# Weight halves at one fixed offset for each kind of stage, in place of offsets that cycle through eight

## The chip, the cores and the metric

The kernel runs on one core of a Trainium2 chip. What counts is the device time of one execution in microseconds (us), taken as the median of several runs. A separate execution is recorded by the hardware profiler; all rows come from that one.

## The reference

One encoder block over 272 token rows (16 learned ones ahead of 256 real ones) of width 2048, in float32:

```python
u = rmsnorm(h, ffn1_pre_g); h = h + 0.5 * rmsnorm(swiglu(u, w_gate, w_up, w_down), ffn1_post_g)
u = rmsnorm(h, mix_pre_g)
z = u @ w_in + b_in                       # 2048 x 9224: both mixers' inputs and two gates
br_m = (sigmoid(mo) * head_rmsnorm(mlstm(q, k, v, i, f))) @ m_w_branch
br_a = head_rmsnorm(diff_attention(aq, ak, av)) @ a_w_branch
h = h + rmsnorm((sigmoid(gm) * br_m + sigmoid(ga) * br_a) @ w_out, mix_post_g)
u = rmsnorm(h, ffn2_pre_g); h = h + 0.5 * rmsnorm(swiglu(u, ...), ffn2_post_g)
return h[:, 16:]
```

The feed-forward width is 5632. Nearly all the work is matrix products of the token rows with weights that are each used once.

## The kernel before

**Float32 products in three passes.** Every weight and every activation is split into a high half H (a copy that TensorE can multiply exactly) and a low half L = value - H. A product is H x XH + H x XL + L x XH. `product` (L202) issues it in one of two forms. Where the rows are 272 wide, three matmuls: L210 (H, XH), L211 (H, XL), L212 (L, XH). Where they are 256 wide and XH and XL lie side by side, two: one 512 wide with H (L215, L217) and one 256 wide with L (L214, L218). The 128 x 128 weight block is loaded anew for each matmul (the PEld rows).

**Units.** The weights come as 377 units of 128 x 2048 values (1 MB), in the order of their use. `load_unit` (L146) fetches the next one by DMA into one of three W tiles (L155), copies its two halves of 1024 columns with ScalarE into H tiles (L166) and lets VectorE subtract for the L tiles (L167). H and L have four tiles each, two of them per unit, so the next unit is split while TensorE works on the present one. A unit holds 16 products: 48 matmuls in the first form, 32 in the second. TensorE takes units strictly in order, so unit n begins with the first matmul of lines L210 to L218 after those of the units before it, and its stretch is read from there to the first matmul of the next.

**Where the halves lie.** An H or L tile is 1088 float32 values a partition (4352 bytes, 17 x 256), of which a unit uses 1024. Where in the tile they start is set by `phase(u)` (L80): for unit u the high half starts at 32 x (u mod 8) bytes and the low one at 32 x ((u + 2 x (u div 8)) mod 8) bytes. A pair of starts comes back every 32 units. The weight blocks within a unit are 512 bytes apart. The rows they meet have pitches that are whole multiples of 256 bytes: 576 values in U (L108), 320 or 256 values in the cells of the feed-forward's middle (L371) and 256 in the mixers' outputs HM and HA (L476, L800). So within one unit the distance from weights to rows is constant, counted modulo 256 bytes. Three small unused tiles (GAPS, L77, L103) set where the pools begin.

**Stages in order.** First feed-forward, 272 rows: 4 units that accumulate four blocks at once (`group`, L237), 44 single blocks (`block`, L267), 24 units of the down projection, 40 blocks, 20 units down. Mixer: 4 units, 5 + 24 blocks on 272 rows and 16 on 256, 8 units of the first branch (`branch`, L733), 32 gate blocks, 8 units of the second branch, 16 for the output projection. Second feed-forward, 256 rows: 4, 44, 24, 40 and 20 units. In the mixer the small matmuls of the attention and the matrix memory are put between units (`advance`).

Of the kernel before, what the change touches and what calls it, by code (L numbers as in the profile page):

```python
# [29 lines left out]
D, SEQ, META, DFF = 2048, 256, 16, 5632  # L30
T = META + SEQ
KT = D // 128
# [44 lines left out]
GAPS = (32, 40, 8)  # L77


def phase(u):  # L80
    h, l = u % 8, (u + 2 * (u // 8)) % 8
    return 8 * h, 8 * l

# [2 lines left out]
def block_kernel(ctx: ExitStack, tc: tile.TileContext, ht_d, w_d, vec_d, con_d, gc_d, out_d):  # L88
# [10 lines left out]
    def f(ap):  # L99
        return ap.bitcast(F32)  # L100
# [40 lines left out]
    def behind(ins, prev):  # L141
        tc.add_manual_dep(ins.ins, prev.ins.name,
                          mybir.DependencyInfo(mybir.DependencyClass.NoSync,
                                               mybir.DependencyReason.DATA), reason="issue order")

    def load_unit(parts=1, hold=None, dma=None):  # L146
        pieces = max(parts, st["pieces"])
        u = unit_no[0]
        unit_no[0] += 1
        W = sp.tile([128, 2048], F32, name="W", bufs=3)  # L150
        hp, lp = phase(u)
        n = 2048 // parts
        for i in range(parts):
            s = slice(i * n, (i + 1) * n)
            st["dma"] = nc.sync.dma_start(W[:, s], w_d[u, :, s])  # L155
            if dma:
                dma(i)
        HL = []
        for i in range(2):
            H = sp.tile([128, 1088], F32R, name="H", bufs=4)[:, hp:hp + 1024]  # L160
            L = sp.tile([128, 1088], F32R, name="L", bufs=4)[:, lp:lp + 1024]
            n = 2048 // pieces
            for o in range(0, 1024, n):
                s = slice(o, o + n)
                w = W[:, 1024 * i + o:1024 * i + o + n]
                a = nc.scalar.activation(H[:, s], w, AF.Copy)  # L166
                b = nc.vector.tensor_sub(L[:, s], w, f(H[:, s]))  # L167
                q = (1024 * i + o) // n
                if hold and hold[q % len(hold)]:
                    for x, y in zip((a, b), hold[q % len(hold)]):  # L170
                        behind(x, y)
            HL.append((H, L))
        return HL

# [7 lines left out]
    def bank(tag):  # L182
        return pp.tile([128, 512], F32, tag=tag, name=tag, bufs=BANKS[tag])

    def mm(cycle=1):
        tag = CYCLE[psn[0] % cycle]
        psn[0] += 1
        return bank(tag)
# [12 lines left out]

    def product(ps, HL, o, X, first, last):  # L202
        turn[0] = False if first else not turn[0]
        H, L = HL[o // 1024]
        o %= 1024
        H, L = H[:, o:o + 128], L[:, o:o + 128]
        XH, XL, both = X
        n = XH.shape[-1]
        if both is None:
            nc.tensor.matmul(ps[:, :n], H, XH, start=first, stop=False)  # L210
            nc.tensor.matmul(ps[:, :n], H, XL, start=False, stop=False)  # L211
            st["mm"] = nc.tensor.matmul(ps[:, :n], L, XH, start=False, stop=last)  # L212
        elif last or turn[0]:
            nc.tensor.matmul(ps[:, :n], L, XH, start=False, stop=False)  # L214
            st["mm"] = nc.tensor.matmul(ps[:, :2 * n], H, both, start=False, stop=last)  # L215
        else:
            nc.tensor.matmul(ps[:, :2 * n], H, both, start=first, stop=False)  # L217
            st["mm"] = nc.tensor.matmul(ps[:, :n], L, XH, start=False, stop=False)  # L218

    def halves(ps, X):  # L220
        n = X[0][0].shape[-1]
        return [ps[:, :n]] if X[0][2] is None else [ps[:, :n], ps[:, n:2 * n]]

    def plain(X):
        return [(h, l, None) for h, l, _ in X]
# [10 lines left out]

    def group(X, nk, n, tail=False, cycle=8, after=None, feed=None):  # L237
        pss = [mm(cycle) for _ in range(4)]
        Xb = [plain(X) if feed else X] * 4
        if tail:  # L240
            Xb[3] = plain(X)
        nu = nk // 4
        splits = []
        st["splits"] = splits
        for u in range(nu):
            if feed:
                hold = None
                if u == 1 and not feed.dma:
                    hold = [(st["square"],)] * 2 + [splits[2]] * 2
                elif u:  # L250
                    hold = [splits[4 * u - 2]]
                HL = load_unit(4 if u < 2 or feed.dma else 1, hold,
                               feed.dma(u) if feed.dma else None)
                splits += [feed(k) for k in range(4 * u, 4 * u + 4)]
            else:
                HL = load_unit()
            order = [(k, b) for k in range(4) for b in range(4)]
            if tail and u == nu - 1:
                order = [(k, b) for b in range(4) for k in range(4)]
            for k, b in order:  # L260
                kk = u * 4 + k
                product(pss[b], HL, k * 512 + b * 128, Xb[b][kk], kk == 0, kk == nk - 1)
                if tail and u == nu - 1 and k == 3 and after:
                    after(b, halves(pss[b], Xb[b]))
        return [halves(p, x) for p, x in zip(pss, Xb)]

    def block(X, cycle=1):  # L267
        ps = mm(cycle)
        HL = load_unit()
        for k in range(KT):  # L270
            product(ps, HL, k * 128, X[k], k == 0, k == KT - 1)
        return halves(ps, X)
# [56 lines left out]
    def residual(yg, r, cols, n, g):  # L329
        def feed(k):  # L330
            if k == 6:
                st["late"]()
            t = tmp()
            a = nc.vector.tensor_mul(t[:, :n], yg[:, k], r[:, :n])
            b = nc.vector.tensor_add(hT[:, k, cols], hT[:, k, cols], t[:, :n])
            if k == 0:
                st["first"] = b
            elif k == 1:
                behind(a, st["first"])
            return prenorm_operand(k, g, cols)  # L340
        feed.dma = None
        return feed
# [21 lines left out]
    def ffn(cols, n, post, feed):  # L364
# [28 lines left out]
        def pair(j):  # L393
            sg = gate(block(X, 8))
            up(j, sg, block(X, 8))

        def down(chunk, nk):
            for g in range(4):
                last = chunk == 1

                def finish(b, ps):
                    k = 4 * g + b
                    for p in ps:
                        nc.vector.tensor_add(Y[:, k], p, Y[:, k])
                    add_square(state["acc"], Y[:, k], n, k)
                    post_scale(Y, k, post)

                pss = group(F, nk, n, tail=last, after=finish if last else None)
                if not last:
                    for b in range(4):  # L410
                        total(Y[:, 4 * g + b], pss[b])

        psn[0] = 0
        pss = group(X, KT, n, feed=feed)
        pss += [block(X, 8) for _ in range(2)]
        state["r"] = rstd_of(prenorm_sum(cols, n), n, "rpre")
        pss.append(block(X, 8))
# [25 lines left out]
    def feed(k):  # L443
        return prenorm_operand(k, "f1pre", ALL)
# [13 lines left out]
    feed = residual(Y, r, ALL, T, "mpre")  # L458
# [274 lines left out]
    def branch(X, finish):  # L733
        for b2 in range(8):
            advance()
            HL = load_unit()
            pss = [mm(4), mm(4)]
            for k in range(8):
                for b in range(2):
                    product(pss[b], HL, k * 256 + b * 128, (X[:, k, 0], X[:, k, 1], X[:, k]),  # L740
                            k == 0, k == 7)
            for b in range(2):
                finish(2 * b2 + b, [pss[b][:, :SEQ], pss[b][:, SEQ:]])

    wide = {"mq", "mk", "mv", "ak", "av"}
# [12 lines left out]
    def advance():  # L758
        with tc.issue_after(st["mm"].ins):
            for g in list(waiting):  # L760
                if next(g, "end") == "end":
                    waiting.remove(g)
            if units:
                begin(units.pop(0))
# [5 lines left out]

    psn[0] = 0
    pss = group(XA, KT, T, feed=feed)
    pss += [start_block(i, 8) for i in (4, 5)]
    st["r"] = rstd_of(prenorm_sum(ALL, T), T, "rpre")
# [13 lines left out]
    def keep(j, ps):  # L788
        total(tm[:, j], ps)

    branch(HM, keep)
    gz = view(slot("G0", SLOTS["G0"], F32), 0, KT, SEQ)
    run(base["gm"], base["ga"])
# [35 lines left out]
    feed = residual(Y2, r, REAL, SEQ, "f2pre")  # L829
# [8 lines left out]
    for k in (2, 0, 6, 4, 10, 8, 12, 14):  # L838
        y, h = Y[:, k:k + 2], hT[:, k:k + 2, REAL]
# [163 lines left out]
```

## Time and profile before

| | us |
|---|---|
| median of 3 runs | 2299.19 (2296.04 to 2299.42) |
| profiled execution | 2298.4 |
| its span, first to last instruction | 2296.5 |
| TensorE matmuls busy | 2279.1 (99%) |
| TensorE weight loads busy | 2101.2 (91%) |
| VectorE busy | 1420.2 (62%) |
| ScalarE busy | 1160.5 (51%) |

Some 1.9 us lie around the span. The mean granted TensorE clock is 0.996 of full speed. A matmul's row shows from its start to its modelled end, and successive ones overlap: a 272-wide one is shown as 289 ns long while the next starts some 125 ns later. What a unit costs is therefore read from starts, not from busy time.

### The profile page before, as it was taken

What the parts mean: (1) busy time and instruction counts of PE and PEld (TensorE: products, weight loads), DVE (VectorE), ACT (ScalarE), POOL (GpSimd) and SP (SyncE); (2) the same over time, 40 slices, a digit from 0 to 9 for tenths busy, and PEclk for the clock granted to TensorE, in tenths of its full rate; (3) what the DMA queues carried; (4) which work ended last, traced back from release to release, by engine and by line L of the source; (5) the groups of instructions that cost most, each with busy time, mean ns of one, the idle gap of its engine ahead of it and who ended that gap; (6) DMA issues with size and microseconds to landing.
All of it is one profiled execution on the core that took longest, in us unless ns stands there. A gap on an engine that the chain in (4) does not pass through costs nothing.

```text
span 2296.5 us, 37068 instructions
## 1 busy us (share of the span) xinstructions
PE 2279.1 (99%) x15325; PEld 2101.2 (91%) x15325; DVE 1420.2 (62%) x2470; ACT 1160.5 (51%) x1869; POOL 0.8 (0%) x5
## 2 busy tenths in 40 slices
PE   9999999999999999999999999999999999999998
PEld 9999999999999998988987888888888888888897
DVE  7555544455555496488588757668666544666655
ACT  6444433444444465555569655556454444454444
POOL 0000000000000000000000000000000000000000
PEclk9999999999999999999999999999999999999999
DMA  7544444544454544434443455545555555555553
GB/s 255 176 179 177 173 181 169 182 168 183 167 183 165 195 178 147 172 123 166 165 147 129 183 184 184 191 157 186 193 189 184 189 193 186 184 186 192 191 184 110
DMA packets 61529, 404.56 MB, mean 176 GB/s; under 512 B 6704, under 2 KB 8880, under 8 KB 14000
## 3 DMA queue, kind: packets, MB, share of 16 engines
q1 hardware_dynamic: 61216, 400.33, 48.7%
q8 instruction: 120, 1.97, 0.3%
q0 software_dynamic: 144, 1.87, 0.2%
q14 instruction: 49, 0.40, 0.0%
HBM read 400.07 MB, written 2.10 MB: 175 GB/s over the span
## 4 chain that ended last, share of the span: by engine, by line
PE 98%; DVE 1%; DMA 0%; ACT 0%; issue 0%; SPq 0%; DVEq 0%
PE mm L215 10%; PE mm L217 10%; PE mm L210 7%; PE mm L212 7%; PE mm L211 7%; PE aux L210 6%; PE aux L212 6%; PE aux L211 6%; PE aux L215 5%; PE aux L217 5%; PE mm L214 5%; PE mm L218 5%; PE aux L214 3%; PE aux L218 3%; PE vt L212 2%; PE vt L211 2%
## 5 line engine op out<-in xcount | busy, mean ns | idle before, releaser
L167 DVE TENSOR_TENSOR L<-W,H 128x1024 fp32r<-128x1024 f32 (+1 forms) x866 | 935.1, 1085 | 610.2 <-ACT H L166 599.3
L166 ACT ACTIVATE H<-W 128x1024 fp32r<-128x1024 f32 (+1 forms) x866 | 812.1, 946 | 768.7 <-PE aux L211 214.6
L210 PE MATMUL mm<-U,H 128*128 128x272 f32 (+1 forms) x1056 | 306.2, 291 | 8.3 <-ACT U L321 7.9
L212 PE MATMUL mm<-U,L 128*128 128x272 f32 (+1 forms) x1056 | 304.4, 289 | 0.4 <-DVE L L167 0.4
L211 PE MATMUL mm<-U,H 128*128 128x272 f32 (+1 forms) x1056 | 304.6, 289 | 0.0
L217 PE MATMUL mm<-U,H 128*128 128x512 f32 x728 | 289.3, 398 | 0.0
L215 PE MATMUL mm<-U,H 128*128 128x512 f32 x728 | 288.2, 396 | 0.0
L210 PE MATMUL aux<-U,H 128*128 128x272 f32 x752 | 217.1, 289 | 0.0
L211 PE MATMUL aux<-U,H 128*128 128x272 f32 x752 | 216.3, 288 | 0.0
L212 PE MATMUL aux<-U,L 128*128 128x272 f32 x752 | 216.2, 288 | 0.0
L210 PEld LDWEIGHTS mm<-U,H 128*128 128x128 f32 x1056 | 199.1, 189 | 10.2 <-ACT U L321 9.2
L214 PE MATMUL mm<-U,L 128*128 128x256 f32 x728 | 205.4, 282 | 0.0
L218 PE MATMUL mm<-U,L 128*128 128x256 f32 x728 | 205.0, 282 | 0.0
L211 PEld LDWEIGHTS mm<-U,H 128*128 128x128 f32 x1056 | 200.0, 189 | 0.8 <-DVE U L322 0.2
L212 PEld LDWEIGHTS mm<-U,L 128*128 128x128 f32 x1056 | 199.7, 189 | 0.9 <-DVE L L167 0.9
L214 PEld LDWEIGHTS mm<-U,L 128*128 128x128 f32 x728 | 137.2, 188 | 32.8 <-issue 0.4
L218 PEld LDWEIGHTS mm<-U,L 128*128 128x128 f32 x728 | 137.3, 189 | 32.0 <-issue 0.7
L217 PE MATMUL aux<-U,H 128*128 128x512 f32 x367 | 145.1, 395 | 0.0
L212 PEld LDWEIGHTS aux<-U,L 128*128 128x128 f32 x752 | 141.7, 188 | 0.0
L211 PEld LDWEIGHTS aux<-U,H 128*128 128x128 f32 x752 | 141.6, 188 | 0.1
L210 PEld LDWEIGHTS aux<-U,H 128*128 128x128 f32 x752 | 141.3, 188 | 0.1
L215 PE MATMUL aux<-U,H 128*128 128x512 f32 x353 | 139.2, 394 | 0.0
(272 smaller groups left out, 4420.3 us busy)
## 6 DMA issues: line engine op xcount, KB each, us to landing
W<-in_w_dram SPq DMA_DIRECT2D x369, 1024.0 KB, 4.8
W<-in_w_dram SPq DMA_DIRECT2D x32, 256.0 KB, 5.3
out_dram<-hT SPq DMA_DIRECT2D x8, 256.0 KB, 2.4
G<-in_gc_dram POOLq DMA_DIRECT2D x1, 1824.0 KB, 8.0
hT<-in_h_dram SPq DMA_DIRECT2D x6, 272.0 KB, 5.4
hT<-in_h_dram SPq DMA_DIRECT2D x1, 544.0 KB, 6.6
con<-in_con_dram SPq DMA_DIRECT2D x1, 528.0 KB, 5.8
vec<-in_vec_dram SPq DMA_DIRECT2D x1, 118.5 KB, 2.0
```

What stands on the lines that cost most here:

```text
L166: a = nc.scalar.activation(H[:, s], w, AF.Copy)
L167: b = nc.vector.tensor_sub(L[:, s], w, f(H[:, s]))
L210: nc.tensor.matmul(ps[:, :n], H, XH, start=first, stop=False)
L211: nc.tensor.matmul(ps[:, :n], H, XL, start=False, stop=False)
L212: st["mm"] = nc.tensor.matmul(ps[:, :n], L, XH, start=False, stop=last)
L214: nc.tensor.matmul(ps[:, :n], L, XH, start=False, stop=False)
L215: st["mm"] = nc.tensor.matmul(ps[:, :2 * n], H, both, start=False, stop=last)
L217: nc.tensor.matmul(ps[:, :2 * n], H, both, start=first, stop=False)
L218: st["mm"] = nc.tensor.matmul(ps[:, :n], L, XH, start=False, stop=False)
```

## The change

The function of the unit number is replaced by a table with one pair of starts, in bytes, for each of four kinds of unit; every unit of a kind uses the same pair. Tiles, DMAs, instructions and their order are as before.

```diff
-def phase(u):
-    h, l = u % 8, (u + 2 * (u // 8)) % 8
-    return 8 * h, 8 * l
+PHASES = {"wide": (192, 0), "narrow": (32, 96), "cells": (64, 64), "dense": (192, 192)}
...
-        hp, lp = phase(u)
+        hp, lp = [p // 4 for p in PHASES[kind]]
...
+        kind = ("wide" if n > SEQ else "narrow") if nk == KT else "cells" if n > SEQ else "dense"
...
-                HL = load_unit()
+                HL = load_unit(kind)
...
     def block(X, cycle=1):
         ps = mm(cycle)
-        HL = load_unit()
+        HL = load_unit("wide" if X[0][0].shape[-1] > SEQ else "narrow")
...
     def branch(X, finish):
         for b2 in range(8):
             advance()
-            HL = load_unit()
+            HL = load_unit("dense")
```

So "wide" is a unit that meets the 272 rows in U, "narrow" one that meets the 256 rows in U, "cells" the first feed-forward's down projection, and "dense" the second one's and the two branches.

## Rows read from the trace of the kernel before

**Rows 1.** The page: chain that ended last (part 4), weight DMAs (part 6).

```profile
PE 98%; DVE 1%; DMA 0%; ACT 0%; issue 0%; SPq 0%; DVEq 0%
...
W<-in_w_dram SPq DMA_DIRECT2D x369, 1024.0 KB, 4.8
```

**Rows 2.** TensorE's waits: engine, line, releaser, us in total, times, longest.

```profile
PE mm L210 <- ACT U L321: 7.9, 2, 4.0
```

**Rows 3.** Windows of TensorE, whole stages: stretch, length, busy (matmuls), clock, DMA share, GB/s.

```profile
440.98:681.59 240.62, 240.62 (x1922) 1.00 0.49 175
296.47:440.98 144.50, 144.50 (x1154) 1.00 0.49 176
1944.61:2168.88 224.27, 224.27 (x1281) 1.00 0.53 187
1810.27:1944.61 134.34, 134.34 (x769) 1.00 0.52 190
2168.88:2275.64 106.76, 106.76 (x685) 1.00 0.44 163
1397.73:1442.56 44.83, 44.83 (x257) 1.00 0.52 184
```

**Rows 4.** Windows of TensorE, one unit each, units 14, 110, 66, 169, 265, 294, 358.

```profile
92.03:97.95 5.92, 5.92 (x50) 1.00 0.51 177
669.63:675.55 5.92, 5.92 (x50) 1.00 0.52 178
404.83:410.75 5.92, 5.92 (x50) 1.00 0.58 216
1066.50:1072.05 5.55, 5.55 (x33) 1.00 0.51 202
1653.28:1658.83 5.55, 5.55 (x33) 1.00 0.50 154
1815.95:1821.47 5.52, 5.52 (x34) 1.00 0.67 233
2174.59:2180.18 5.60, 5.60 (x38) 1.00 0.58 224
```

**Rows 5.** Windows of TensorE, one unit each, units 8, 40, 205, 227, 168.

```profile
55.85:61.86 6.00, 6.00 (x50) 1.00 0.77 281
248.25:254.33 6.08, 6.08 (x50) 1.00 0.49 174
1307.92:1313.58 5.66, 5.66 (x33) 1.00 0.50 190
1431.34:1436.97 5.63, 5.63 (x33) 1.00 0.55 191
...
1060.65:1066.50 5.85, 5.85 (x35) 1.00 0.65 251
```

**Rows 6.** Timeline within unit 14: start, length, engine, line, what.

```profile
92.16 1.06 ACT L166 ACTIVATE H<-W 128x1024 fp32r<-128x1024 f32 x1 [1.94 <-PE aux L211]
...
92.77 0.28 PE L210 MATMUL aux<-U,H 128*128 128x272 f32 x1
...
93.14 0.29 PE L210 MATMUL aux<-U,H 128*128 128x272 f32 x1
...
96.21 1.22 DVE L167 TENSOR_TENSOR L<-W,H 128x1024 fp32r<-128x1024 f32 x1 [1.38 <-ACT H L166]
...
96.47 0.28 PE L210 MATMUL aux<-U,H 128*128 128x272 f32 x1
...
96.84 0.29 PE L210 MATMUL aux<-U,H 128*128 128x272 f32 x1
...
97.58 0.29 PE L210 MATMUL aux<-U,H 128*128 128x272 f32 x1
...
97.95 0.29 PE L210 MATMUL aux<-U,H 128*128 128x272 f32 x1
```

**Rows 7.** A window of TensorE in the mixer, columns as in rows 3.

```profile
879.60:886.40 6.80, 6.80 (x25) 0.50 0.04 14
```

More of the change, by code (lines that the diff above doesn't have):

```diff
@@ L144, in behind, with load_unit @@
                                                mybir.DependencyReason.DATA), reason="issue order")
-    def load_unit(parts=1, hold=None, dma=None):
+    def load_unit(kind, parts=1, hold=None, dma=None):
         pieces = max(parts, st["pieces"])
@@ L251, in group @@
                     hold = [splits[4 * u - 2]]
-                HL = load_unit(4 if u < 2 or feed.dma else 1, hold,
+                HL = load_unit(kind, 4 if u < 2 or feed.dma else 1, hold,
                                feed.dma(u) if feed.dma else None)
```

## The prediction

> **What bounds the kernel now.** I read the chain of work that ended last first: 98% of it is TensorE [rows 1]. The list of TensorE's waits comes next. Its largest entry is 7.9 us in two waits, the two places where a new set of token rows is normalised [rows 2]; against a span of 2296.5 us TensorE hardly ever waits. So only the pace at which matmuls follow one another can give time back, and that pace doesn't show in busy time, which is the whole of every stretch. It shows in how long one unit of 16 products takes from its first matmul to the next unit's first. Third, therefore, I cut whole stages and single units out with the windows view. The count in brackets identifies a unit: 48 matmuls for a wide unit or cells, 32 for a narrow or dense one (36 where one of four blocks takes separate passes), and one or two more whose modelled ends reach in from before.
>
> The kernel before gives its units 32 pairs of starts in turn, and all four pairs of the new table are among them: the starts are 32 x h and 32 x l bytes, and (192, 0) is h, l = (6, 0), (32, 96) is (1, 3), (64, 64) is (2, 2), (192, 192) is (6, 6). From the formula, (6, 0) falls on units 14, 46, 78, 110 and 174, of which the first and fourth stand in [rows 4]; (2, 2) meets cells in units 66 and 130, (1, 3) meets narrow rows in units 169, 201, 233, 265 and 329, and (6, 6) meets dense cells in units 294 and 358. The trace of before holds small samples of the kernel after.
>
> **The change part by part.** No instruction is added, removed or moved. A unit still costs one DMA, the same copies and subtractions, and the same matmuls, in tiles of the same size at the same places. What changes is the address of the weight halves inside their tiles, and so the pace of the matmuls that read them. Each term below is (mean unit of an undisturbed stage less the unit at the table's pair) times the number of such units.
>
> Wide: 240.62 us for 40 units is 6.0155 [rows 3]; at (6, 0) it is 5.92, both early and 578 us later [rows 4]. 0.0955 us apiece. There are 121 wide units; the first of each of the two feed-forward and mixer openings follows operands that are still being made and I leave them out. 119 x 0.0955 = 11.4 us.
>
> Cells: 144.50 us for 24 units is 6.021 [rows 3]; at (2, 2) 5.92 [rows 4]. 44 x 0.101 = 4.4 us.
>
> Narrow: 224.27 us for 40 units is 5.607 [rows 3]; at (1, 3) 5.55, in the mixer and in the second feed-forward [rows 4]. 147 units in the two-matmul form x 0.057 = 8.4 us.
>
> Dense: 134.34 us for 24 units is 5.598 and at (6, 6) 5.52, so 24 x 0.078 = 1.9 us. The last down projection takes 106.76 us for its first 19 units, 5.619 each, and at (6, 6) 5.60: 20 x 0.02 = 0.4 us [rows 3, 4].
>
> Two sizes the trace doesn't show. The 16 branch units never had (6, 6). Their second set takes 44.83 us for 8, mean 5.604 [rows 3], and its dearest unit is 5.63 [rows 5]. At worst (6, 6) is as dear as that one, a loss of 16 x 0.026 = 0.4 us; at best as cheap as 5.52, a gain of 16 x 0.084 = 1.3 us. Rows and weights are laid out there as in the second down projection, 256 values of XH beside 256 of XL at pitches that are multiples of 256 bytes, so I take that projection's difference, 16 x 0.078 = 1.2 us. The five narrow units in three matmuls (four after the mixer, one in the output projection) never had (1, 3) either. The spread of wide units, 6.08 less 5.92 [rows 4, 5], bounds them at 5 x 0.16 = 0.8 us either way; I take nothing.
>
> The sum is 11.4 + 4.4 + 8.4 + 1.9 + 0.4 + 1.2 = 27.7 us. Against the profiled execution's 2298.4 us (span 2296.5 and 1.9 around it) that gives 2298.4 - 27.7 = **2270.7 us**. The median of the runs, 2299.19, is 0.8 above that execution, and its fastest run 2.4 below; I make no allowance.
>
> All of it lies on the path, since nothing but TensorE is there. What would be late next? A weight DMA lands in 4.8 us [rows 1], and the DMA engines are 0.53 busy in the narrow stage [rows 3], while the shortest new unit is 5.52 us. Splitting takes ScalarE two copies of 1.06 us and VectorE two subtractions of 1.22 us in a wide unit [rows 6]. None of these reaches 5.5 us, so the gain isn't handed to another engine.
>
> One thing moves with time alone. In the mixer TensorE's granted clock is at its lower level (0.50, 1.2 GHz) for 6.8 us after a run of small gate matmuls [rows 7]; the products of a narrow unit lie in it and lose about half of it, 3.4 us. The change brings that place forward by some 13 us (95 wide and 44 cells units lie ahead of it). The spell could be shorter or longer, so 3.4 us either way goes into the range, which is also how far the three runs lie apart.
>
> **A rule that speaks against it.** Unit 8 and unit 14 do the same work on the same rows with the same full clock and differ only by where the halves start, 6.00 against 5.92 [rows 4, 5]. The Trainium skill, "TensorE: Matmul & The Clock Gate", section "Step-by-step: what each phase is for", holds that TensorE reads streamed rows and weights through two independent ports, so that "Loading the next tile's weights doesn't steal SBUF read bandwidth from the running matmul". By that rule the sum would be nothing; by the rows it is 27.7 us. The trace disagrees with the rule as far as these units go.
>
> **The rivals.**
>
> *A slower rhythm locks in.* The same pair doesn't always give the same time: (0, 2) gave 6.00 in unit 8 and 6.08 in unit 40 [rows 5], each steady over its 48 matmuls, so the rhythm that a unit inherits matters. Before, the pair changes after 6 us and a bad rhythm dies; after, 40 units in a row could keep it. With 0.08 us lost in every wide and cells unit, 163 x 0.08 = 13.0, the time would be 2283.7. Against it: both wide samples at (6, 0) and the cells at (2, 2) come to the same 5.92, which looks like a floor, and unit 169 takes its 5.55 right after unit 168, in which other matmuls stood between the products (35 counted, 5.85 us) [rows 4, 5]. Chance 0.12.
>
> *The distance isn't the cause.* A pair recurs every 32 units, so PSUM bank, tile number and the preceding pair recur with it, and the difference could belong to one of those. With any distance then alike, nothing is gained and the time is 2298.4. For it: every (6, 0) sample follows a (5, 7) unit. Against it: units 14 and 66 have different pairs ahead of them, different rows and different destinations, and both are at 5.92; unit 8 at 6.00 has no other work than unit 14. The skill's rule above would make this the outcome. Chance 0.03.
>
> *Slower: the writes come to the same place as the reads.* While TensorE reads one unit's halves, ScalarE and VectorE write the next one's. Before, the next H starts 32 bytes on from the present one, and since h and l of a unit always differ by an even number of steps, an H write never had the start of a half being read. After, every write within a kind has the start of the half now read. If that slowed TensorE while they write, 2 x 1.06 + 2 x 1.22 = 4.6 of 5.9 us, by as much as the dearest distance costs (0.16 a wide unit, and 5.66 less 5.55 a narrow one [rows 4, 5]), the loss is 0.78 x (165 x 0.16 + 212 x 0.11) = 38.8 us and the time 2298.4 - 27.7 + 38.8 = 2309.5. It decides from 27.7 / 377 = 0.07 us a unit. Against it: a write passes through all starts in turn, and in unit 14 the products start 0.37 us apart under a ScalarE write (92.77 to 93.14), under a VectorE one (96.47 to 96.84) and with neither (97.58 to 97.95) [rows 6]. Chance 0.04.
>
> **How the numbers follow.** Forecast 0.81, slower rhythm 0.12, distance not the cause 0.03, slower 0.04. The forecast's own range is the sum with its unknowns: 2270.7 less 3.4, 0.8 and 0.1 is 2266.4 below; above, plus 3.4, 0.8 and 1.6 (branches as dear as they can be) 2276.5. Rounding of rows to 0.01 us is 377 x 0.005 = 1.9 us more on either side, 2264 to 2278. A part of the slower rhythm (in one long stage or two) belongs within 8 times in 10, so the range is 2264 to 2281. A measurement of this kernel can tell 0.2%, 4.6 us, from no change. The forecast and the slower rhythm are both faster by more: 0.93. Same 0.03, slower 0.04.
>
> **What would show it.** Right: every undisturbed wide unit and every cells unit at 5.92, narrow 5.55, the second feed-forward's first down projection 5.52; the stage that was 240.62 us at 236.8, the one of 224.27 at 222.0, the one of 134.34 at 132.5; no new entry in TensorE's waits. Wrong: wide units steady at 6.0 or more (a slower rhythm, or not the distance), or matmuls that stretch just while L166 or L167 runs (the writes).

## The result and the profile after

The changed kernel takes 2273.85 us (median of 4 runs, 2273.77 to 2274.42), the kernel before 2299.1. The ratio is 0.9894, 95% interval 0.9881 to 0.9906. Forecast were 2270.7 us and a range of 2264 to 2281. The profiled execution takes 2273.8 us with a span of 2272.0: 24.5 us less than before, where the sum had 27.7.

Part 4 of the page is as it was, 98% TensorE, and the longest entry of TensorE's waits too [rows 2]. One entry is new, a single wait of 0.2 us. In the kernel after, the lines up to L238 have moved up by one, so L209 is the former L210.

```profile
PE mm L209 <- ACT U L321: 7.9, 2, 4.0
...
PE mm L210 <- DVE U L322: 0.2, 1, 0.2
```

The windows of TensorE over the same stages (columns as in [rows 3]; stretch, length, busy with count of matmuls, clock, DMA share, GB/s). The first six answer to [rows 3] in its order. Then come the second feed-forward's first 44 units, the mixer's first 4 wide units and its first 8 narrow ones.

```profile
434.26:671.07 236.80, 236.80 (x1922) 1.00 0.50 178
292.18:434.26 142.09, 142.09 (x1154) 1.00 0.50 178
1922.73:2144.61 221.88, 221.88 (x1281) 1.00 0.53 189
1790.04:1922.73 132.69, 132.69 (x769) 1.00 0.53 191
2144.61:2251.10 106.49, 106.49 (x685) 1.00 0.46 164
1379.24:1423.56 44.31, 44.31 (x257) 1.00 0.52 184
1543.45:1790.04 246.59, 246.59 (x1412) 1.00 0.53 190
795.35:822.27 26.91, 26.90 (x192) 0.89 0.39 138
852.82:906.55 53.73, 53.73 (x294) 0.97 0.48 165
```

The last three stretches in the kernel before, and the two spells at the lower clock that [rows 7] doesn't show:

```profile
1563.26:1810.27 247.01, 247.01 (x1412) 1.00 0.53 189
807.71:833.71 26.01, 26.00 (x192) 0.93 0.39 142
864.81:920.64 55.83, 55.83 (x294) 0.94 0.44 159
...
807.90:811.31 3.41, 3.41 (x15) 0.50 0.25 107
1538.36:1541.77 3.41, 3.41 (x16) 0.50 0.02 5
```

What to see: the 40 wide units went from 240.62 to 236.80 us, 5.920 each, where 236.8 had been forecast. Cells 144.50 to 142.09, the later 40 narrow units 224.27 to 221.88 (forecast 222.0), dense 134.34 to 132.69 (132.5). But the earlier 44 narrow units, which ought to have gained 2.5, gained 0.4.

The windows of single units show why: unit 265 and unit 330, the same kind, rows and pair.

```profile
1633.24:1638.84 5.60, 5.60 (x33) 1.00 0.50 176
1994.84:2000.39 5.55, 5.55 (x33) 1.00 0.57 204
```

The timeline of TensorE inside each (start, length, engine, line), first of the stage at 5.60 and then of the one at 5.55:

```profile
1639.54 0.39 PE L216 MATMUL aux<-U,H 128*128 128x512 f32 x1
...
1640.24 0.40 PE L216 MATMUL aux<-U,H 128*128 128x512 f32 x1
1640.48 0.28 PE L217 MATMUL aux<-U,L 128*128 128x256 f32 x1
1640.60 0.28 PE L213 MATMUL aux<-U,L 128*128 128x256 f32 x1
1640.71 0.39 PE L214 MATMUL aux<-U,H 128*128 128x512 f32 x1
1640.94 0.39 PE L216 MATMUL aux<-U,H 128*128 128x512 f32 x1
...
1994.84 0.39 PE L216 MATMUL aux<-U,H 128*128 128x512 f32 x1
1995.07 0.28 PE L217 MATMUL aux<-U,L 128*128 128x256 f32 x1
1995.19 0.28 PE L213 MATMUL aux<-U,L 128*128 128x256 f32 x1
1995.31 0.39 PE L214 MATMUL aux<-U,H 128*128 128x512 f32 x1
1995.54 0.39 PE L216 MATMUL aux<-U,H 128*128 128x512 f32 x1
```

Four matmuls take 0.70 us in both; the difference is a few ns in each, so it needs a whole unit to be seen. From start to start, to the nanosecond and from the same trace, the spacings come back every eight matmuls (one round; this is the rhythm): 236, 118, 116, 228, 232, 117, 119, 234 ns in the slow stage (1400 in all) and 230, 118, 116, 230, 229, 118, 116, 230 (1387) in the other. All units from 252 to 292 take 5.600 us, those of the later 40 5.546 to 5.553. Unit 265 had taken 5.55 before, at the same pair [rows 4]. This looks like a rhythm that was inherited and then kept, the rival that was given 0.12, in one stage of the many. The first experiment tests it.

### The profile page after: what moved, and what is told of

Same layout as the page of the kernel before. It is cut to its first block, busy times and chain, and to the rows that moved or that the text cites. A ratio compares the mean times of both kernels' runs of the same rounds, so it can differ in the third digit from the quotient of the medians.

```text
span 2272.0 us, 37068 instructions
## 1 busy us (share of the span) xinstructions
PE 2254.3 (99%) x15325; PEld 2082.1 (92%) x15325; DVE 1419.5 (62%) x2470; ACT 1159.6 (51%) x1869; POOL 0.8 (0%) x5
## 4 chain that ended last, share of the span: by engine, by line
PE 98%; DVE 1%; DMA 0%; ACT 0%; issue 0%; SPq 0%; DVEq 0%
PE mm L214 10%; PE mm L216 10%; PE mm L211 7%; PE mm L209 7%; PE mm L210 7%; PE aux L211 6%; PE aux L209 6%; PE aux L210 6%; PE aux L214 5%; PE aux L216 5%; PE mm L213 5%; PE mm L217 5%; PE aux L213 3%; PE aux L217 3%; PE vt L211 2%; PE vt L209 2%
## 5 line engine op out<-in xcount | busy, mean ns | idle before, releaser
L209 PE MATMUL mm<-U,H 128*128 128x272 f32 (+1 forms) x1056 | 304.4, 289 | 8.3 <-ACT U L321 7.9
L210 PE MATMUL mm<-U,H 128*128 128x272 f32 (+1 forms) x1056 | 302.3, 287 | 0.2 <-DVE U L322 0.2
L209 PE MATMUL aux<-U,H 128*128 128x272 f32 x752 | 214.8, 286 | 0.0
L210 PE MATMUL aux<-U,H 128*128 128x272 f32 x752 | 214.3, 285 | 0.0
L209 PEld LDWEIGHTS mm<-U,H 128*128 128x128 f32 x1056 | 199.5, 189 | 10.3 <-ACT U L321 9.2
L210 PEld LDWEIGHTS mm<-U,H 128*128 128x128 f32 x1056 | 199.6, 189 | 0.8 <-DVE U L322 0.4
L209 PEld LDWEIGHTS aux<-U,H 128*128 128x128 f32 x752 | 141.3, 188 | 0.1
L210 PEld LDWEIGHTS aux<-U,H 128*128 128x128 f32 x752 | 141.0, 188 | 0.1
```

## The experiments

All are edits of the changed kernel. Stages are compared in the profiled executions.

**One unit at another pair.** The rows are the whole stage, then units 252, 253 and 292.

```diff
+KICK = {252: (0, 64)}
...
-        hp, lp = [p // 4 for p in PHASES[kind]]
+        hp, lp = [p // 4 for p in KICK.get(u, PHASES[kind])]
```

> The changed kernel, but unit 252 alone, early in the second feed-forward's first 44 narrow units, starts its halves at (0, 64) bytes. In the changed kernel units 252 to 292 all take 5.600 us although the same pair takes 5.547 in the later 40 narrow units. If that is a slower rhythm inherited from the stage's start, one unit at another distance breaks it: units 253 to 292 at 5.547, the stage's 44 units 2.1 us shorter, time 2271.7 us. If the slow rhythm belongs to the stage (its rows, its DMAs), it comes back at once: units 253 to 292 at 5.600, time 2273.9.

```profile
1544.95:1789.45 244.50, 244.50 (x1412) 1.00 0.52 190
...
1561.94:1567.58 5.64, 5.64 (x33) 1.00 0.36 118
1567.58:1573.13 5.55, 5.55 (x33) 1.00 0.52 195
1783.90:1789.45 5.55, 5.55 (x33) 1.00 0.61 216
```

The odd unit itself costs 5.64, the next one 5.55 and so do the 39 after it: the stage takes 244.50 us, 2.1 less, as the inherited rhythm foretold. Nothing in the stage's rows or DMAs holds it slow. The time fell less than that, to 2273.04 us (0.9886 of before, 0.9872 to 0.9901). In its profiled execution the spell at the lower clock that begins at 1518 us lasts 6.8 us where the changed kernel has 3.4, and the four units there take 25.96 us for 25.11; the mixer's first 8 narrow units take 0.3 more.

**Rows moved, weights not.**

```diff
-    gap(cp, 0)
     rows = cp.tile([128, KT, ROW], F32R, name="U")
+    gap(cp, 0)
```

> The changed kernel, but the gap of 128 bytes ahead of the row tile U lies behind it: U starts 128 bytes lower, everything else stays where it was, the weights' starts too. If the distance from weights to rows sets the pace, wide units meet the distance of the old pair (64, 128), 6.03 to 6.04 us before, and narrow ones that of the old (160, 224), 5.66; cells (5.92) and the dense down projection (5.52) don't read U and stay. Time 2273.9 + 119 x 0.115 + 147 x 0.11 = 2304. If the start of the weights in itself sets it (which place of the memory they are read from), nothing changes: 2273.9.

Wide, narrow, cells and dense stages:

```profile
439.33:680.40 241.07, 241.07 (x1922) 1.00 0.48 175
1945.06:2171.72 226.66, 226.66 (x1281) 1.00 0.51 186
297.24:439.33 142.09, 142.09 (x1154) 1.00 0.49 179
1812.37:1945.06 132.69, 132.69 (x769) 1.00 0.53 191
```

The first 19 units of the last down projection, whose rows didn't move either:

```profile
2171.72:2278.63 106.91, 106.91 (x685) 1.00 0.45 163
```

The weights are read from the very same places as in the changed kernel. Wide units go from 5.920 to 6.027 and narrow ones from 5.547 to 5.667, while cells and dense units, whose rows didn't move, keep 142.09 and 132.69 to the last digit. Time 2301.34 us (one run), above the kernel before; of the 2304 expected the wide units stayed short (0.107 dearer and not 0.115), and so did the earlier 44 narrow ones (2.9 us dearer and not 4.8), which had been in the slow rhythm already. It is not where the weights lie, but where they lie against the rows. The last fence shows what distance doesn't explain: 106.91 us for the changed kernel's 106.49, most units at 5.627 for 5.600, with nothing moved that they read. That looks like a slower rhythm in a second stage; no run tested it.

**Rows and weights moved together.** As the last one, and

```diff
-PHASES = {"wide": (192, 0), "narrow": (32, 96), "cells": (64, 64), "dense": (192, 192)}
+PHASES = {"wide": (64, 128), "narrow": (160, 224), "cells": (64, 64), "dense": (192, 192)}
```

> As the run with U 128 bytes lower, and the wide and narrow weights start 128 bytes further on too, modulo 256: wide (64, 128), narrow (160, 224). By distance the old relation is back: wide 5.92, narrow 5.55 (5.60 where the slower rhythm holds), time 2271 to 2276. By the start of the weights in itself, these are the pairs that cost 6.03 and 5.66 in the kernel before: about 2304.

```profile
434.40:671.22 236.83, 236.83 (x1922) 1.00 0.49 178
1921.55:2143.41 221.87, 221.87 (x1281) 1.00 0.52 189
1544.53:1788.89 244.36, 244.36 (x1412) 1.00 0.53 192
2143.41:2250.28 106.87, 106.87 (x685) 1.00 0.46 163
```

The old times are back, 2273.41 us (one run). The wide high half went 128 bytes down and the low one 128 up, so the distance counts modulo 256 bytes. In the third row the earlier narrow stage is in the fast rhythm without an odd unit. Up to two matmuls of L277, which stand at the seam of units 250 and 251, its rounds of eight take 1400 ns from the stage's second on, as in the changed kernel; behind them they take 1387 here and 1400 there. Unit 251 of the changed kernel, then units 251 and 252 of this run:

```profile
1554.66:1560.44 5.78, 5.78 (x34) 1.00 0.58 211
...
1555.74:1561.48 5.74, 5.74 (x34) 1.00 0.58 236
1561.48:1567.03 5.55, 5.55 (x33) 1.00 0.30 93
```

The fourth row, the last down projection, is slower than in the changed kernel again, as in the run before.

**One fixed pair, the dearest.**

```diff
-PHASES = {"wide": (192, 0), "narrow": (32, 96), "cells": (64, 64), "dense": (192, 192)}
+PHASES = {"wide": (128, 192), "narrow": (160, 224), "cells": (128, 128), "dense": (160, 160)}
```

> The changed kernel with one fixed pair for each kind, but the dearest one seen in the trace of before: wide (128, 192), 6.08 us; narrow (160, 224), 5.66; cells (128, 128), 6.08; dense (160, 160), 5.68. If the gain is the choice of distance, the time is 2273.9 + 163 x 0.16 + 147 x 0.11 + 60 x 0.1 = 2322, some 23 above the kernel before. If holding any distance fixed brings the gain (no unit has to start in another's rhythm), it stays near 2274 to 2280.

```profile
445.86:689.05 243.19, 243.19 (x1922) 1.00 0.48 173
299.94:445.86 145.91, 145.91 (x1154) 1.00 0.48 174
1959.17:2185.83 226.66, 226.66 (x1281) 1.00 0.52 185
1824.10:1959.17 135.07, 135.07 (x769) 1.00 0.52 189
```

6.07 to 6.08 for every wide and cells unit of these stages, 5.667 for most narrow ones: 2316.61 us (2316.51 to 2320.55), 1.0082 of before (1.0065 to 1.0099). To keep one distance is worth nothing in itself; a fixed bad one is dearer than the cycle, which averages over all. The miss against 2322 is mostly narrow: the earlier 44 units rose by 2.9 us instead of 4.8, since they had been in the slow rhythm already, and the mixer's first 8 fell to 53.08 us instead of rising by 0.9, because there is no spell at the lower clock there in this run (of the clock below).

**A map of pairs.**

```diff
+MAP = _map()
...
-        hp, lp = [p // 4 for p in PHASES[kind]]
+        hp, lp = [p // 4 for p in MAP.get(u, PHASES[kind])]
```

> A map, not a candidate: in the long stages every unit has a pair of its own. Wide units 7 to 47 and 72 to 94 go through all 64 pairs of 32-byte steps, narrow units 253 to 292 and 317 to 340 too, cells and dense units through the 32 pairs whose two starts differ by an odd number of steps (the kernel before never had those), and what units are left try starts 4, 8 and 16 bytes off the table's pair. If weights and rows collide by distance, the even pairs repeat the times of the trace before, (192, 0) at 5.92 and (32, 96) at 5.55, and the odd ones lie in the same 5.92 to 6.09 and 5.54 to 5.68. If the table's pairs are the best there are, nothing is below 5.92 for wide and cells and 5.54 for narrow. If the low half's start counted alone (it is read once in three matmuls, the high one twice), a row of the map with one high start would show a spread of a third of the whole, and a column with one low start two thirds; if only the distance of each half to the rows counted, the map would be a sum of a high part and a low part.

Wide units 79 at (192, 0), 107 at (196, 0), 86 at (192, 224), and narrow unit 355 at (40, 104):

```profile
483.77:489.70 5.92, 5.92 (x50) 1.00 0.50 173
651.91:657.88 5.97, 5.97 (x50) 1.00 0.50 178
525.64:531.72 6.08, 6.08 (x50) 1.00 0.54 183
2151.03:2156.58 5.55, 5.55 (x33) 1.00 0.48 180
```

Of the 32 pairs that the kernel before had, 30 wide and 28 narrow ones repeat a time of its trace within 0.02 us, though each stands behind another pair here than there. The six others are 0.02 to 0.07 us off, so a single unit's time carries that much of what went before it. Of the 64 wide pairs (192, 0) alone is at 5.92; the mean is 6.017, that of the old cycle (6.0155). Narrow ones lie between 5.55 and 5.68, as expected, three of the 64 at 5.55. Cells at the 24 odd pairs that were tried in the first down projection lie between 5.97 and 6.09, dense units at the same pairs between 5.57 and 5.71: nothing is below the table's pairs there. No sum of a high part and a low part describes the map: the best such sum leaves 0.031 of the 0.037 us of scatter among wide units. The surprise is the second row: 4 bytes off is already 0.05 us dearer. Each such time comes from one unit, but the three wide units within 4 bytes all took 5.97 or more. So the wide pair is a point, not the middle of a broad good place. The narrow one is less alone: with both halves 8 or 16 bytes further on a unit took 5.549 or 5.555 (fourth row), with one half alone 8 or 16 bytes off 5.57 to 5.65. The execution took 2291.64 us.

**The version that follows from this.** The odd unit 252 of the first experiment, and a pair of its own for the 20 units of the last down projection, taken from unit 374 of the trace before.

```diff
...
+          "last": (192, 64)}
+KICK = {252: (0, 64)}
...
+        kind = ("wide" if n > SEQ else "narrow") if nk == KT else "cells" if n > SEQ else "last" if tail else "dense"
```

> The changed kernel with two more pairs: unit 252 alone at (0, 64), as in the run that broke the slow rhythm, and the 20 units of the last down projection at (192, 64), where unit 374 of the kernel before took 5.53 us against 5.60 at the table's (192, 192). By distance and inherited rhythm: the second feed-forward's first 44 units 244.5 us (from 246.6), the last 20 units 1.3 us shorter (112.1 to 110.8), time some 3.4 below the changed kernel's on the same chip, about 2270.5. If unit 374's 5.53 was only a passing rhythm, the last stage stays at 112.1 and the time is about 2272.

```profile
1543.35:1787.85 244.50, 244.50 (x1412) 1.00 0.53 191
2142.38:2247.56 105.18, 105.18 (x685) 1.00 0.46 166
```

2270.35 us (2269.47 to 2271.59), 0.9877 of before (0.9862 to 0.9891). The last stage's first 19 units fell from 106.49 to 105.18. The changed kernel, timed beside it:

> The changed kernel again, on the same chip as the version with two more pairs, so that a difference of 0.1% can be told: 2273.9 us, as measured, and the second feed-forward's first 44 units again at 5.600 if the slow rhythm comes with the program and not with the run.

```profile
1543.28:1789.87 246.59, 246.59 (x1412) 1.00 0.52 190
```

2274.29 us (2273.64 to 2275.21), 0.9895 of before (0.9878 to 0.9911). The slow rhythm came back in the same stage with the same 246.59 us, so it comes with the program. The runs of the two don't overlap: the version is 3.9 us faster, of which the two stages account for 2.09 + 1.35 = 3.4 in the profiled executions.

## Why the prediction was right, and what it had wrong

*TensorE's pace is the bound, and nothing else is late next.* Right: the waits are unchanged but for the new one of 0.2 us, and the differences of the units add up to the span's 24.5 us.

*Wide, 11.4 us.* The long stages gave what was forecast, 0.095 a unit. The mixer's 29 wide units after its first four gave 2.3 us instead of 2.8 (presumably not every pair of the cycle falls on them alike). The four first ones lost 0.9, by the clock (below). Measured 9.5 in all 121 units.

*Cells, 4.4.* Measured 4.2, every undisturbed unit at 5.920.

*Narrow, 8.4.* This is the term whose price was wrong. The later 40 units gave 2.4, the gates and the output projection what was forecast; the mixer's first 8 gave 2.1, of which 1.6 by the clock; the first 44 of the second feed-forward gave 0.4 for 2.5. The pair alone was priced, from units that each stood behind another pair. Held over 41 units, the same pair kept a rhythm 0.053 us slower, and the one unit that broke it gave the 2.1 us back. Measured 8.0 in all, 6.4 without the clock: that it ends so near the forecast is luck.

*Dense, 1.9 + 0.4 + 1.2.* Measured 1.65, 0.3 and 0.9. One unit at 5.52 had stood for all 24 of the first; the first and the last unit of each group of four blocks took 5.53 to 5.57. The branches, which the trace of before couldn't show, came to 5.54 in their second set: the guess from the down projection had the sign and most of the size.

*Separate-pass narrow units, nothing.* The output projection's last unit and the four after the mixer differ by less than 0.05 us.

*The clock, 3.4 us either way.* The spells exchanged places. The prediction looked at the one after the gates alone; the one behind the first feed-forward changed as well. Before, the one behind the first feed-forward lasted 3.4 us and the one after the gates 6.8 [rows 7]; after, 6.8 and 3.4:

```profile
794.58:801.41 6.83, 6.06 (x26) 0.50 0.39 141
869.67:873.08 3.41, 3.41 (x13) 0.50 0.00 0
1518.20:1521.61 3.41, 3.26 (x15) 0.50 0.02 5
```

So 4 wide units rose from 26.01 to 26.91 us and 8 narrow ones fell from 55.83 to 53.73, 1.6 more than their distance gives. Together that is some 0.4 us for the change, within the 3.4. What sets the length of a spell stays open. The changed kernel timed again shows 6.8 and 3.4 us at the same two places, the run with the dearest pairs no spell after the gates at all.

*The sum, 27.7 us.* It was 3.2 too high: 2.1 by the slower rhythm, some 1.5 by smaller shortfalls of the other terms, and 0.4 came back by the clock.

*Rivals.* The slower rhythm came true in one long stage, a narrow one, and cost 2.1 us, not 13. That distance isn't the cause is refuted by the rows moved alone and moved with the weights: at the same clock and work, the distance alone moves a wide unit from 5.920 to 6.027 us. The Trainium skill, "TensorE: Matmul & The Clock Gate", section "Step-by-step: what each phase is for", holds that loading the next weights doesn't take read bandwidth from the running matmul. By that rule moving the rows would have changed nothing. These runs don't bear it out for the float32 operands used here. That writes at the same place slow the reads is refuted by 236.80 us for 40 units, all of them under such writes.

What stays open is which two accesses meet. The rows moved show that it is the place of the weights against that of the rows. The writing of the next halves seems not to be one of the two: in unit 80 of the run with the dearest pairs each of the eight rounds of six matmuls takes 760 ns, also where no half is being written (496.94 to 497.65 us). Whether a weight load waits for the stream or the other way round isn't in the rows.

## What to carry to other kernels

Where an engine is 99% busy and never waits, its pace may still depend on where its operands lie; here it was up to 3%. If a kernel cycles through placements, its trace is already the experiment: group the units by placement before building anything. And a sample taken in a mixed sequence prices the placement, not the rhythm that a long uniform run settles into; look for two prices at one placement, and see whether one odd unit changes them.

## What the hardware showed that was not expected

- The times come in steps. In their second half 41 of the map's 64 wide units run at a pace of 5.920, 5.973, 6.027 or 6.080 us a unit, 0.053 apart: 6.7 ns each time the pattern of six matmuls comes round, eight times a unit. Narrow units step by 0.027 us, 6.7 ns in each of four rounds of eight (1387, 1393, 1400, 1407 and 1413 ns).
- A rhythm can outlive a break. In the changed kernel units 250 and 251 took 5.84 and 5.78 us because the matmuls of L277 stood in between, and unit 252 went on at 5.600; one unit at another distance ended it. The same break did end it in the run with rows and weights both moved, at the same distances, so which of the two happens isn't explained.
- Starts 4 bytes apart differ: 5.92 at (192, 0), 5.97 at (196, 0), the latter from one unit.
